# Splitting a weight tile whole instead of in two halves in a decoder step's projection queue

## The chip, the cores and the metric

The kernel runs on one core of one Trainium2 chip. The metric is device time in microseconds (us) of one execution; lower is better. Three runs of the kernel before gave a median of 2542.75 us (2541.96 to 2546.72).

## What is computed

One inference step of a two-layer decoder for 288 tokens (256 of a prompt, 32 of samples), in float32. Each layer has a token mixer and then a channel mixer. The token mixer multiplies the tokens by a wide weight matrix, runs three recurrent branches (mLSTM, GLA, SSD) on the result, projects each branch, gates and adds them, and applies an output matrix:

```python
z = jnp.matmul(x, w_in).astype(f32)
...
proj = jnp.einsum('blnc,ncd->blnd', br, w_branch.astype(f32))
gates = jax.nn.sigmoid(gate.reshape(B, L, N_BRANCH, D_MODEL))
mixed = jnp.sum(gates * proj, axis=2)
y = jnp.matmul(mixed, w_out.astype(f32))
h = _layernorm(DN_ALPHA * x.astype(f32) + y, ln1_g, ln1_b)
h = _layernorm(DN_ALPHA * h + _peer(h, p_wq, p_keys, p_u, p_v), ln2_g, ln2_b)
```

The change touches the weight matrices of the token mixer (`w_in`, `w_branch`, `w_out`). The channel mixer (`_peer`) is left as it is.

## The kernel before

A float32 product is made of three products of a shorter format. Every operand x is split into a high part (x copied into the short format, on ScalarE, L209) and a low part (x minus the high part, on VectorE, L210). TensorE adds up high times high, high times low and low times high.

The token mixers of both layers get their weights through one queue, `self.jobs`. A weight tile has 8 blocks of 128 x 128. It is loaded as a whole into a ring of `NRAW` = 3 buffers `raw` (L215, on the queue of SyncE) and used as two jobs of 4 blocks each. A layer has 83 such tiles, so 166 jobs. A job is 12 matmuls: for each block one with the high part of the weights and the high part of the tokens (L324), one with the high part of the weights and the low part of the tokens (L326), one with the low part of the weights (L328). Two jobs add up one output tile `pz` in PSUM; behind its last matmul stands `done(ps)`, which takes the output away (convolution, gate, mix and so on).

`feed()` is a generator that issues one matmul per step. The branches (`ssd`, `mlstm`, `gla`) issue their own work and call `pump(n)` in between, which takes n steps of the generator. In the mixers the engines' order is the order of issue (`tc.manual_schedule()`), so each engine works through its instructions just as this interleaving writes them; the stage after it is ordered by the planner.

At the start of job k the generator sees to it that jobs k to k + `NHI` - 1 (`NHI` = 4) are split. `hilo` splits half a tile: one buffer `hl` of the ring of four holds the high part of the half in its first 4 blocks and the low part in the last 4. `whole` splits a whole tile at once and takes two buffers of the same ring, one for the high parts of all 8 blocks and one for the low parts. The channel mixer uses `whole` (the products of `proj`, the tiles of `in_v`); the first weight tile of each layer's mixer is split as two halves by `prefetch` and `presplit`. A buffer of the ring is free again when the last matmul that reads it is done. At the end of the mixer `leave` hands the tiles that are loaded and not yet used to the channel mixer.

Names that the text uses: `convolve` (L539 to L555: two copies and one scaled copy on ScalarE, three multiply-adds on VectorE L545, and for the tile before a sigmoid L551 on ScalarE and two products L553, L555 on VectorE), `sigmoids` (L488), `gate_r` (L481), `mix` (L511, L512), `merge` (L1250, L1252, L1255).

Of the kernel before, what the change touches and what calls it, by code (L numbers as in the profile page):

```python
# [69 lines left out]
class Kernel:  # L70
# [225 lines left out]
    def add_z(self, j, done):  # L296
        self.add_x(self.I["win"][self.L, j], self.xh, self.xl, done)

    def feed(self):
        k = 0  # L300
        raws, parts = self.raws, self.parts = {}, {}
        for i, (r, p) in enumerate(self.ahead):
            raws[i] = r
            parts.update({2 * i + h: x for h, x in enumerate(p) if x})
        self.ahead = []
        ps = None
        while True:
            while k >= len(self.jobs):
                yield 0

            self.loaded = min((k + NHI) // 2 + NRAW, len(self.jobs) // 2) * 2
            for i in range(k, self.loaded):
                if i // 2 not in raws:
                    raws[i // 2] = self.load(self.jobs[i][0])
                if i < k + NHI and i not in parts:
                    parts[i] = self.hilo(raws[i // 2], i % 2)
            hi, lo = parts.pop(k)
            _, operands, done = self.jobs[k]
            first = ps is None
            if first:  # L320
                ps = self.ps_pj("pz")[:, :T]
            for m, (xh, xl) in enumerate(operands):
                last = m == 3 and done is not None
                self.pe.matmul(ps, hi[:, m], xh, start=(first and m == 0), stop=False)  # L324
                yield 1
                self.pe.matmul(ps, hi[:, m], xl, start=False, stop=False)  # L326
                yield 1
                self.pe.matmul(ps, lo[:, m], xh, start=False, stop=last)  # L328
                if last:
                    done(ps)  # L330
                    ps = None
                yield 1
            self.jobs[k] = None
            k += 1
            self.fed = k // 2
# [1507 lines left out]
```

## Time and profile before

| | |
|---|---|
| median of 3 runs | 2542.75 us (2541.96 to 2546.72) |
| the profiled execution, device time | 2553.09 us |
| its span from first to last instruction | 2551.3 us |
| TensorE (PE) busy | 2457.7 us, 96% |
| VectorE (DVE) busy | 1935.7 us, 76% |
| ScalarE (ACT) busy | 1328.5 us, 52% |
| mean granted TensorE clock | 0.979 |

The span has four stages: the mixer of layer 1 (0 to 428 us), its channel mixer (to 1264), the mixer of layer 2 (to 1696), its channel mixer (to 2551). In the timeline a row tells start, duration, engine, line, operation, what is written and read, the shape, and in brackets how long the engine sat idle before it and who released it. A row that ends in "x2" or "x4" is that many instructions behind one another, with their duration in all. Ends of matmuls are modelled.

### The profile page before, as it was taken

The numbers are of one execution on the slowest core, as the hardware profiler recorded it, in microseconds if no ns is written. First come the engines' busy times: TensorE is split into PE (matmuls) and PEld (weight loads), VectorE is DVE, ScalarE is ACT, GpSimd is POOL, SyncE is SP. The second block draws the span as 40 slices with busy tenths as digits, with TensorE's granted clock in tenths as the row PEclk, the third lists the DMA queues.
The fourth block names the chain that finished last, engine by engine and source line by source line (L and its number), as shares of the span: only waits on it lengthen the run. The fifth ranks groups of instructions, "written<-read, shape, count | busy, mean of one in ns | idle before, by whom it ended". The sixth has DMA issues, their size and how long they took to land. (4 is left out here: it accounts for less than half of the span.)

```text
span 2551.3 us, 45304 instructions
## 1 busy us (share of the span) xinstructions
PE 2457.7 (96%) x17014; PEld 2235.0 (88%) x17014; DVE 1935.7 (76%) x4156; ACT 1328.5 (52%) x2675; POOL 269.9 (11%) x270
## 2 busy tenths in 40 slices
PE   8998998989999999999999999989899999999998
PEld 8987897989999988777789888889899999878886
DVE  7667666699778868888676776767997787688885
ACT  6444765445554444444564457653455544444544
POOL 0000100240000012222000001003300000122210
PEclk9999999999999999999999989999999999999999
DMA  4422543546545568888544225434455455688883
GB/s 163 136 92 82 183 143 111 166 143 190 167 163 166 162 216 304 313 305 300 167 134 137 83 88 188 146 111 163 157 183 166 161 164 165 234 308 311 311 281 132
DMA packets 132028, 465.10 MB, mean 182 GB/s; under 512 B 15360, under 2 KB 17536, under 8 KB 131808
## 3 DMA queue, kind: packets, MB, share of 16 engines
q1 hardware_dynamic: 109728, 385.14, 45.4%
q0 software_dynamic: 22080, 77.06, 9.0%
q8 instruction: 134, 2.20, 0.3%
q14 instruction: 86, 0.70, 0.1%
HBM read 451.32 MB, written 10.82 MB: 181 GB/s over the span
## 5 line engine op out<-in xcount | busy, mean ns | idle before, releaser
L210 DVE TENSOR_TENSOR hl<-raw,hl 128x1024 fp32r<-128x1024 f32 (+1 forms) x842 | 844.8, 1008 | 393.3 <-ACT hl L209 382.5
L209 ACT ACTIVATE hl<-raw 128x1024 fp32r<-128x1024 f32 (+1 forms) x880 | 778.2, 888 | 461.4 <-PE pu L254 144.6
L1555 PE MATMUL acc<-hl,wh 128*128 128x512 f32 x2048 | 648.3, 396 | 2.6 <-ACT hl L209 1.4
L253 PE MATMUL pu<-hh,hl 128*128 128x256 f32 x2048 | 504.5, 287 | 12.4 <-ACT WA L1472 12.2
L254 PE MATMUL pu<-hl 128*128 128x256 f32 x2048 | 494.9, 280 | 0.0
L1555 PEld LDWEIGHTS acc<-hl,wh 128*128 128x128 f32 x2048 | 384.7, 188 | 100.5 <-ACT hl L209 4.9
L1555 PE MATMUL acc<-hl,wl 128*128 128x512 f32 x1024 | 404.9, 395 | 0.0
L253 PEld LDWEIGHTS pu<-hh,hl 128*128 128x128 f32 x2048 | 388.2, 190 | 14.1 <-ACT WA L1472 13.3
L254 PEld LDWEIGHTS pu<-hl 128*128 128x128 f32 x2048 | 387.8, 189 | 0.0
L326 PE MATMUL pz<-xl,hl 128*128 128x288 f32 x1008 | 325.0, 322 | 0.6 <-DVE xl L1663 0.3
L324 PE MATMUL pz<-xh,hl 128*128 128x288 f32 x1008 | 308.5, 306 | 11.8 <-ACT xh L209 6.8
L328 PE MATMUL pz<-xh,hl 128*128 128x288 f32 x1008 | 306.7, 304 | 0.0
L256 PE MATMUL pu<-hh,hl 128*128 128x256 f32 x2048 | 284.8, 282 | 2.3 <-DVE hl L210 2.3
L256 PEld LDWEIGHTS pu<-hh,hl 128*128 128x128 f32 x2048 | 260.0, 189 | 3.1 <-DVE hl L210 3.0
L1555 PEld LDWEIGHTS acc<-hl,wl 128*128 128x128 f32 x1024 | 192.5, 188 | 45.7
L209 ACT ACTIVATE wh<-WA 128x256 fp32r<-128x256 f32 x200 | 83.6, 418 | 269.1 <-PE acc L1555 266.7
L326 PEld LDWEIGHTS pz<-xl,hl 128*128 128x128 f32 x1008 | 197.4, 196 | 16.7 <-issue 11.5
L324 PEld LDWEIGHTS pz<-xh,hl 128*128 128x128 f32 x1008 | 197.6, 196 | 14.5 <-ACT xh L209 7.4
L328 PEld LDWEIGHTS pz<-xh,hl 128*128 128x128 f32 x1008 | 198.4, 197 | 3.7 <-issue 2.7
L1676 POOL DMA_INDIRECT gbuf<-in_u,se x64 | 61.7, 964 | 963.3 <-PE pu L256 701.0
L210 DVE TENSOR_TENSOR wl<-WA,wh 128x256 fp32r<-128x256 f32 x200 | 84.3, 422 | 48.4 <-ACT wh L209 48.2
L210 POOL TENSOR_TENSOR hl<-raw,hl 128x1024 fp32r<-128x1024 f32 (+1 forms) x38 | 89.6, 2357 | 188.2 <-ACT hl L209 165.6
(584 smaller groups left out, 3366.0 us busy)
## 6 DMA issues: line engine op xcount, KB each, us to landing
raw<-in_ut SPq DMA_DIRECT2D x256, 512.0 KB, 3.5
raw<-in_v SPq DMA_DIRECT2D x256, 512.0 KB, 4.7
raw<-in_win SPq DMA_DIRECT2D x126, 512.0 KB, 3.6
raw<-in_wq SPq DMA_DIRECT2D x32, 512.0 KB, 3.5
raw<-in_wbr SPq DMA_DIRECT2D x24, 512.0 KB, 3.5
raw<-in_wout SPq DMA_DIRECT2D x16, 512.0 KB, 3.6
CS<-in_C SPq DMA_DIRECT2D x16, 256.0 KB, 3.9
out_sC<-CS POOLq DMA_DIRECT2D x16, 256.0 KB, 2.8
```

The costliest lines, as they stand in the source:

```text
L209: self.ac.activation(hi, r, AF.Copy)
L210: (eng or self.ve).tensor_tensor(lo, r, hi.bitcast(F32), op=OP.subtract)
L253: self.pe.matmul(ps, wh[k], self.xh[:, k, :n], start=(k == 0), stop=False)
L254: self.pe.matmul(ps, wh[k], self.xl[:, k, :n], start=False, stop=False)
L256: self.pe.matmul(ps, wl[k], self.xh[:, k, :n], start=False, stop=(k == 7))
L324: self.pe.matmul(ps, hi[:, m], xh, start=(first and m == 0), stop=False)
L326: self.pe.matmul(ps, hi[:, m], xl, start=False, stop=False)
L328: self.pe.matmul(ps, lo[:, m], xh, start=False, stop=last)
L1555: pe.matmul(acc[t][d], lhs[:, 128 * t:128 * t + 128], rhs, start=False, stop=last and n == 2, skip_group_check=True)
L1676: self.gp.indirect_dma_start(out=g, out_offset=None, in_=src, in_offset=bass.IndirectOffsetOnAxis(ap=ix[:, r:r + 1], axis=0))
```

## The change

In `feed`, only at an even k and only for an even i, the tile of jobs i and i + 1 is split by one call of `whole` instead of two calls of `hilo` in two steps. The two jobs then get views of the two buffers: blocks 0 to 3 for job i, 4 to 7 for job i + 1. Number and order of the matmuls, of the loads and of the buffers stay.

```diff
@@ -313,7 +314,10 @@
                 if i // 2 not in raws:
                     raws[i // 2] = self.load(self.jobs[i][0])
                 if i < k + NHI and i not in parts:
-                    parts[i] = self.hilo(raws[i // 2], i % 2)
+                    if i % 2 or k % 2:
+                        continue
+                    w = self.whole(raws[i // 2])
+                    parts.update({i + h: [x[:, 4 * h:4 * h + 4] for x in w] for h in range(2)})
             hi, lo = parts.pop(k)
             _, operands, done = self.jobs[k]
             first = ps is None
```

## Rows read from the trace of the kernel before

**Rows 1.** The page: busy time of each engine; issues of weight loads.
```profile
PE 2457.7 (96%) x17014; PEld 2235.0 (88%) x17014; DVE 1935.7 (76%) x4156; ACT 1328.5 (52%) x2675; POOL 269.9 (11%) x270
...
raw<-in_win SPq DMA_DIRECT2D x126, 512.0 KB, 3.6
```
**Rows 2.** Busy time by stretch (length; PE, PEld, DVE, ACT, POOL; clock): both mixers.
```profile
0.00:428.00 428.00, 392.41 (x2811) 361.47 (x2811) 301.51 (x672) 239.97 (x548) 24.77 (x54) 0.97 0.41 133
...
1264.00:1696.00 432.00, 403.64 (x2862) 370.29 (x2860) 301.94 (x635) 248.16 (x570) 28.33 (x49) 0.95 0.40 129
```
**Rows 3.** Groups by line and shape: halves in 0:428, whole tiles in 450:1250.
```profile
L209 ACT ACTIVATE hl<-raw 128x512 fp32r<-128x512 f32 x170 | 104.4, 624 | 56.5 <-PE pz L328 48.5 <-DMA raw<-in_win 5.3 <-ACT hl L209 1.5
...
L210 DVE TENSOR_TENSOR hl<-raw,hl 128x512 fp32r<-128x512 f32 x170 | 114.5, 687 | 71.5 <-ACT hl L209 70.7
...
L209 ACT ACTIVATE hl<-raw 128x1024 fp32r<-128x1024 f32 x259 | 273.0, 1054 | 175.5 <-PE pu L254 74.4 <-issue 43.9 <-DMA raw<-in_wq 15.3
...
L210 DVE TENSOR_TENSOR hl<-raw,hl 128x1024 fp32r<-128x1024 f32 x241 | 294.8, 1224 | 114.2 <-ACT hl L209 109.3 <-ACT WA L1472 0.7 <-PE pu L256 0.5
```
**Rows 4.** Timeline of PE in the convolution stretch, layer 1.
```profile
30.96 0.29 PE L328 MATMUL pz<-xh,hl 128*128 128x288 f32 x1
...
31.36 0.29 PE L328 MATMUL pz<-xh,hl 128*128 128x288 f32 x1
...
34.54 0.30 PE L328 MATMUL pz<-xh,hl 128*128 128x288 f32 x1
```
**Rows 5.** Busy time by stretch: the convolution stretch, layer 1.
```profile
22.00:38.00 16.00, 16.00 (x121) 15.92 (x120) 15.45 (x35) 12.60 (x30) 0.00 (x0) 1.00 0.42 148
```
**Rows 6.** Timeline of ACT, then of DVE, in the same stretch.
```profile
31.29 0.39 ACT L539 ACTIVATE xp<-pz 128x256 f32<-128x256 f32 x1 [0.64 <-PE pz L328]
...
31.80 0.65 ACT L543 ACTIVATE cv<-xp,par 128x312 f32<-128x312 f32 x1
...
32.71 1.14 ACT L209 ACTIVATE hl<-raw 128x512 fp32r<-128x512 f32 x2
...
31.67 0.42 DVE L553 TENSOR_TENSOR xs<-cv,cvx 128x256 f32<-128x256 f32 x1
...
32.11 1.28 DVE L210 TENSOR_TENSOR hl<-raw,hl 128x512 fp32r<-128x512 f32 x2
33.31 1.70 DVE L545 SCALAR_TENSOR_TENSOR cv<-xp,par,cv 128x312 f32<-128x312 f32 x3
34.93 0.42 DVE L553 TENSOR_TENSOR bcs<-cv,cvx 128x256 f32<-128x256 f32 x1
```
**Rows 7.** Timeline of ACT and PE: splits behind the convolution's table load.
```profile
21.33 1.14 ACT L209 ACTIVATE hl<-raw 128x512 fp32r<-128x512 f32 x2
...
21.76 0.29 PE L328 MATMUL pz<-xh,hl 128*128 128x288 f32 x1
```
**Rows 8.** Timeline of ACT and PE: splits behind the sigmoids of the gates.
```profile
265.76 0.62 ACT L209 ACTIVATE hl<-raw 128x512 fp32r<-128x512 f32 x1
...
266.73 0.30 PE L328 MATMUL pz<-xh,hl 128*128 128x288 f32 x1
...
343.74 2.17 ACT L209 ACTIVATE hl<-raw 128x512 fp32r<-128x512 f32 x4
...
344.40 0.61 PE L324 MATMUL pz<-bmh,hl 128*128 128x288 f32 x1 [3.77 <-ACT hl L209]
...
345.13 0.61 PE L328 MATMUL pz<-bmh,hl 128*128 128x288 f32 x1
```
**Rows 9.** Timeline of DVE and PE: the split behind the last mixes.
```profile
391.34 1.29 DVE L210 TENSOR_TENSOR hl<-raw,hl 128x512 fp32r<-128x512 f32 x2
...
391.96 0.30 PE L328 MATMUL pz<-mh,hl 128*128 128x288 f32 x1
```
**Rows 10.** Timeline of DVE and PE: end of the mixer (merge).
```profile
411.75 0.69 DVE L210 TENSOR_TENSOR hl<-raw,hl 128x512 fp32r<-128x512 f32 x1 [0.21 <-ACT hl L209]
412.36 1.54 DVE L1250 SCALAR_TENSOR_TENSOR xT<-pm,xT 128x288 f32<-128x288 f32 x4
...
413.53 0.75 PE L1255 MATMUL pvar<-sqn,ones 128*128 128x288 f32 x2 [0.39 <-ACT sqn L1252]
```
**Rows 11.** Timeline of PE: SSD's first product.
```profile
55.83 0.30 PE L599 MATMUL pt<-ident,rs 128*128 128x128 f32 x1 [2.71 <-ACT rs L581]
```
**Rows 12.** Busy time by stretch: GLA and mLSTM side by side, layer 1.
```profile
176.00:236.00 60.00, 51.66 (x389) 41.89 (x389) 45.76 (x101) 24.87 (x68) 3.29 (x6) 0.91 0.21 75
```

## Prediction, made before the changed kernel was run

> **What bounds the kernel now.** I began with the page. TensorE is busy 96% of the span, VectorE 76%, ScalarE 52% [rows 1], so the end is set by matmuls one behind the other, and what the change does to the other two engines counts only where TensorE waits for them. Next came the stretches: the change acts in the two mixers alone, and there TensorE is idle for 428 - 392 = 36 us in layer 1 and 28 us in layer 2 [rows 2]. These 64 us are all that a faster split could ever give back; most of them end on the branches. Then came the shapes: a half costs 0.624 us on ScalarE and 0.687 us on VectorE, a whole tile 1.054 and 1.224 us [rows 3]. Last I went through the timeline of the mixers tile by tile and asked, at each tile, when its second half was split and when TensorE wanted the tile's first low part. That comparison decides the case, because the second half's place in the program is the place of the whole split after the change.
>
> **The change part by part.** *What goes away.* For each of about 82 tiles a layer one ScalarE and one VectorE instruction disappear. Added durations say 2 x 0.624 - 1.054 = 0.19 us saved on ScalarE and 2 x 0.687 - 1.224 = 0.15 us on VectorE [rows 3]; started back to back, two halves take VectorE 33.31 - 32.11 = 1.20 us [rows 6], so the saving there may be near nothing. Per layer that is at most 16 and 12 us of engines that mostly have room. It reaches TensorE where VectorE is full, the convolution stretch (15.45 of 16 us busy [rows 5]): six tiles at 0.15 us, at most 0.9 us a layer. I take zero.
>
> *What moves.* Before, the first half of a tile was split three jobs ahead of use and the second half three jobs ahead of its own use. Now the whole tile is split two jobs ahead: the split may start when the tile before the one in work has been used up (its two buffers come free), and has one tile's time. In clean running a tile takes TensorE 34.54 - 31.36 = 3.18 us, and the first low matmul comes 31.36 - 31.25 = 0.11 us behind the end of the tile before [rows 4], so the low part is wanted 3.29 us after its buffers come free. The split takes about 0.35 us until ScalarE has taken away the output ahead of it (one such copy lasts 0.39 us [rows 6]), then 1.05 + 0.04 + 1.22 us: 2.66 us. So 0.6 us is left, where a half had 1.59 us more time and 0.96 us less work. Any other work above 0.6 us that ScalarE or VectorE has in line ahead of the split now stops TensorE. Queued behind the waiting low split on VectorE are the branches' instructions and the next `done`; the weight load of three tiles later waits on SyncE for the same buffer, but that buffer is freed only 0.5 us later, the load lands in 3.6 us [rows 1] and is wanted 9.5 us later, so it costs nothing.
>
> *Convolution stretch.* A tile ends at 31.25. ScalarE starts on it at 31.29 and has the scaled copy at 32.45, 1.2 us behind the end [rows 4, 6]. VectorE then has the three multiply-adds, 34.93 - 33.31 = 1.62 us, two products, 32.11 - 31.67 = 0.44 us [rows 6], and now the whole low part, 1.22 us [rows 3]: 4.48 us behind the end, against 3.29 us wanted. With halves it was 1.2 + 1.62 + 0.44 + 0.69 = 3.95 us against 3.29 + 1.59 = 4.88 us, and TensorE never waited, busy 16.0 of 16 us [rows 5]. The loop closes over two tiles: two tiles take at least 4.48 + 0.04 - 0.11 + 3.18 = 7.59 us where they took 6.36, so every second tile is 1.2 us late. Six tiles stand behind convolutions; the second of them has a table load ahead of its split on ScalarE: high part from 21.33, so low part at 21.33 + 1.05 + 0.04 + 1.22 = 23.64, wanted at 21.76 [rows 7], 1.9 us late; two more are late by 1.2 us. Sum 4.3 us a layer.
>
> *Splits that come late anyway.* Behind the gates' sigmoids ScalarE reaches a split at 265.76; the low part is then there at 268.07 where TensorE wanted it at 266.73 [rows 8]: 1.4 us. At 343.74 four halves are in line; the low part comes at 346.05, wanted at 345.13 [rows 8]: 0.95 us, and the same line of four comes twice in a layer, so 1.9 us. Behind the last mixes the second half's low part began at 391.34, so its high part began at 391.34 - 0.04 - 0.62 = 390.68; the whole low part is there at 392.99, wanted at 391.96 [rows 9]: 1.05 us.
>
> *Chains that a longer split delays.* In `merge` the first tile handed to the channel mixer is now split whole ahead of the centring: its low part begins 0.43 us later and takes 0.6 us longer, so L1250 begins up to 1.0 us later than 412.36, and TensorE already waits 0.39 us for what comes of it [rows 10]: between 0 and 1.0 us, I take 0.8, since that wait shows no cover. SSD's first product waits 2.71 us for a chain through VectorE and ScalarE [rows 11]; a tile's split ahead of that chain is late by over 1 us, but hidden in the wait, and the chain itself gets 0.53 us longer (1.22 - 0.69): 0.5 us. Other tiles with less than 1 us to spare: between 0 and 3 us, I take 1.0, as most of them are late by the 0.3 us that is left between 0.6 and 0.9.
>
> *Sum.* 4.3 + 1.4 + 1.9 + 1.05 + 0.8 + 0.5 + 1.0 = 11 us a layer; layer 2 runs the same program with the same order, 2862 matmuls in 432 us [rows 2], so 22 us. The profiled execution took 2553 us, which would become 2575 us; it stands 10 us above the median of the runs, 2542.75 us, so the median becomes 2565 us. If all that is not in the convolution stretch were hidden, 9 us would stay; with the upper bounds (3.0 for the small places, 1.0 for merge, and 1.2 at SSD's start if its wait covers nothing) it is 14 us a layer, 28 us.
>
> **The rivals.** *No change.* TensorE's own waits (36 and 28 us) swallow the new ones. It needs chains that do not depend on the delayed tiles. For it: the 2.71 us at SSD's start. Against it: the convolution tiles stand ahead of every branch and delay each chain along with the matmuls. It would leave 0 to 5 us, about 2545 us.
>
> *Faster.* VectorE stood idle 71.5 us in layer 1 ahead of its 170 half splits, nearly all for ScalarE's high part [rows 3]. Half of these places go. Where GLA and mLSTM run side by side, TensorE is idle 8.3 of 60 us [rows 12] and the branches' instructions stand behind those splits. That stretch is 60/428 of the mixer: 0.5 x 71.5 x 0.14 = 5 us a layer if it all reached TensorE, and no tile were late: 10 us, 2533 us. It decides from the point at which what these chains win exceeds the new waits, 11 us a layer, so it needs most of the lateness above to be wrong too. The Trainium skill's page "Perfetto Trace Analysis", section "Optimizing Scalar/DVE Operations", speaks for it: larger operations can improve throughput if the engine is saturated, by about 60 ns an instruction on VectorE and 93 ns on ScalarE. Applied to the six tiles of the full stretch, that is an estimate of 0.4 us a layer, which the rows' 0 to 0.15 us a tile bear out. The same section says that splitting instructions up can help where these engines are not saturated but cause bubbles on others; by that rule the change goes the wrong way in most of the mixer, which is what the late tiles above come to.
>
> *Slower still.* TensorE's granted clock. In the stretch where it is often idle the mean is 0.91 [rows 12], in the full one 1.00 [rows 5]; the lower of its two levels, 1.2 against 2.4 GHz, is then granted for part of the time. If the convolution stretch and the tiles around the late splits, some 100 us a layer, fell to 0.91 too, that would be another 9 us a layer: 22 + 18 = 40 us, 2583 us.
>
> **How the numbers follow.** Forecast, slower by about 22 us (9 to 28): 0.66. Slower still, by the clock: 0.15. No change: 0.11. Faster: 0.08. A measurement of this kernel can tell about 0.2%, 5 us. So slower 0.81, same 0.11, faster 0.08. The range leaves out the faster case and the top of the clock's: 2546 to 2581 us.
>
> **What would show it.** In the profile after, the group of the split is 128x1024 in the mixers too, some 164 fewer instructions on either engine. In the stretch from 20 to 45 us TensorE has gaps ahead of L328 (low part, released by VectorE L210) of about 1.9, 1.2 and 1.2 us, which were not there; the groups L324 and L328 of `pz` show idle time ended by `hl`, together some 15 to 20 us. Each mixer is 9 to 14 us longer, the channel mixers unchanged. Wrong would be: no gaps at L328 in the convolution stretch (then the two-tile loop is wrong), gaps but no later end of the mixer (absorbed), or a shorter stretch at 176 to 236 us (the queue on VectorE was worth more than thought).

## The result and the profile after

The changed kernel took 2585.64 us (median; 2581.28 to 2587.13), the kernel before 2544.73 us (2541.96 to 2553.18): ratio 1.0146, 95% interval 1.0125 to 1.0168. Slower was right; 2565 us was not, and 2585.64 us lies above the range. Beside the experiments the kernel before was run many more times, with medians of 2547.5 to 2548.9 us, so the change costs 37 to 41 us.

The page of the kernel after, the lines that answer to [rows 1, 3, 4]. The lines of the feed stand four lower than before, so L332 is the matmul with the low part that was L328, and L328 the one that was L324. In a group, "|" is followed by busy time, mean ns of one, and the idle time ahead with what ended it.

```profile
PE 2464.9 (96%) x17014; PEld 2239.7 (87%) x17014; DVE 1920.8 (74%) x3988; ACT 1300.8 (50%) x2507; POOL 264.0 (10%) x270
...
L210 DVE TENSOR_TENSOR hl<-raw,hl 128x1024 fp32r<-128x1024 f32 (+1 forms) x674 | 823.6, 1223 | 394.1 <-ACT hl L209 376.7
...
L332 PE MATMUL pz<-xh,hl 128*128 128x288 f32 x1008 | 308.0, 306 | 13.1 <-DVE hl L210 13.1
L328 PE MATMUL pz<-xh,hl 128*128 128x288 f32 x1008 | 306.8, 304 | 9.7 <-ACT xh L209 5.9
```

VectorE and ScalarE issue 168 instructions fewer each and are busy 15 and 28 us less, yet the time rose. In the group L332 TensorE now waits 13.1 us for low parts. The same group on the page of the kernel before had no wait:

```profile
L328 PE MATMUL pz<-xh,hl 128*128 128x288 f32 x1008 | 306.7, 304 | 0.0
```

In the convolution stretch, where it never stopped [rows 5], the timeline of PE of the kernel after has these waits in layer 1 (the first three of four; in brackets the idle time and who ended it):

```profile
16.62 0.40 PE L332 MATMUL pz<-xh,hl 128*128 128x288 f32 x1 [0.53 <-DVE hl L210]
...
21.06 0.40 PE L332 MATMUL pz<-xh,hl 128*128 128x288 f32 x1 [0.73 <-DVE hl L210]
...
28.81 0.40 PE L332 MATMUL pz<-xh,hl 128*128 128x288 f32 x1 [0.98 <-DVE hl L210]
```

To see where the rest went I cut each mixer at the ends of tiles 0, 13, 53 and 82, so that each stretch holds the same matmuls in every kernel. First come the busy times by stretch of the kernel after (columns as in [rows 2]; three stretches of layer 1, then three of layer 2), then those of the kernel before with two buffer counts lowered, which is the control of the experiments and took the same time as the kernel before.

```profile
12.45:65.29 52.84, 45.99 (x319) 43.59 (x318) 40.26 (x94) 28.92 (x52) 0.00 (x0) 0.97 0.42 130
65.29:313.80 248.51, 232.49 (x1695) 206.33 (x1695) 161.40 (x327) 122.64 (x270) 13.82 (x25) 0.95 0.38 115
313.80:432.44 118.64, 109.32 (x765) 106.12 (x765) 78.41 (x135) 65.08 (x123) 3.77 (x7) 0.96 0.46 148
1299.46:1349.65 50.19, 44.76 (x319) 42.39 (x318) 35.06 (x61) 29.00 (x52) 0.00 (x0) 1.00 0.45 137
1349.65:1597.50 247.85, 231.95 (x1695) 206.33 (x1695) 156.14 (x296) 122.58 (x270) 13.83 (x25) 0.95 0.38 115
1597.50:1716.00 118.50, 109.19 (x765) 105.98 (x765) 78.40 (x135) 65.11 (x123) 3.78 (x7) 0.96 0.47 148
```

```profile
14.28:61.08 46.80, 44.06 (x319) 43.66 (x318) 40.57 (x107) 30.52 (x65) 0.00 (x0) 0.96 0.46 147
61.08:298.83 237.75, 224.35 (x1695) 200.56 (x1695) 165.92 (x368) 127.64 (x309) 13.85 (x25) 0.99 0.39 120
298.83:412.32 113.49, 108.10 (x765) 104.92 (x765) 81.09 (x164) 70.05 (x151) 3.78 (x7) 0.97 0.47 155
1280.71:1324.70 43.99, 42.57 (x319) 42.16 (x318) 35.10 (x76) 30.48 (x65) 0.00 (x0) 1.00 0.48 154
1324.70:1568.70 244.00, 230.57 (x1695) 205.74 (x1695) 161.21 (x338) 127.99 (x309) 13.87 (x25) 0.96 0.37 118
1568.70:1682.14 113.44, 108.05 (x765) 104.87 (x765) 81.08 (x164) 70.04 (x151) 3.79 (x7) 0.97 0.48 155
```

The lengths add up to 836.5 us after and 799.5 us in the control: 37.1 us. The rest of the span is 6.0 us shorter in the profile after (spans 2579.4 and 2548.3 us), so it is partly chance that this agrees so well with the 37 us of the medians. Length less TensorE's busy time is its idle time: 62.8 against 41.8 us, 21.1 us more. The other 16.0 us are the same matmuls taking longer. Part of that belongs to the waits: a matmul is drawn 0.29 us long and the next begins 0.13 us behind it [rows 4], so at a wait the last one still counts as busy for 0.16 us, and the one behind it takes 0.40 us; a wait costs some 0.27 us more than its bracket says. The rest is the granted clock: in these stretches the trace has its lower level, 1.2 GHz, for 44 us in the control, 61 us in the profile of before and 72 us after. The same cut through the profile of the kernel before gives 802.4 us, 37.4 of it idle. By stretch, both layers together:

| us | tiles 1 to 13 | tiles 14 to 53 | tiles 54 to 82 | sum |
|---|---|---|---|---|
| control | 90.8 | 481.8 | 226.9 | 799.5 |
| the profiled execution of before | 91.3 | 485.4 | 225.8 | 802.4 |
| after | 103.0 | 496.4 | 237.1 | 836.5 |
| predicted to be added | 9.6 | 4.8 | 7.5 | 21.9 |
| added, against the control | 12.2 | 14.6 | 10.2 | 37.1 |
| added, against before | 11.7 | 11.0 | 11.4 | 34.1 |

The middle, where the branches run, is where the added time is furthest from the forecast. Two things are in it: longer waits for the branches' chains of instructions, and slower matmuls. One chain shows the first. These are rows of ACT, DVE and PE from the timeline of the kernel before, then of the kernel after: GLA's state update, for which TensorE waits at `pr`. The bracket of the last row tells how long TensorE was idle and for what.

```profile
282.90 0.41 ACT L474 ACTIVATE gate<-pz 128x288 f32<-128x288 f32 x1 [1.85 <-PE pz L328]
283.20 0.62 ACT L209 ACTIVATE hl<-raw 128x512 fp32r<-128x512 f32 x1
...
283.86 0.69 DVE L210 TENSOR_TENSOR hl<-raw,hl 128x512 fp32r<-128x512 f32 x1 [2.09 <-ACT hl L209]
284.47 0.68 DVE L924 TENSOR_TENSOR CS<-CS,ec 128x512 f32<-128x512 f32 x1
...
285.26 0.69 DVE L925 TENSOR_TENSOR CS<-CS,pc__3121 128x512 f32<-128x512 f32 x1
...
286.09 1.10 PE L1173 MATMUL pr<-sq,ones 128*128 128x512 f32 x2 [0.42 <-DVE CS L925]
```

```profile
290.62 0.41 ACT L478 ACTIVATE gate<-pz 128x288 f32<-128x288 f32 x1 [3.23 <-PE pz L332]
290.93 1.05 ACT L209 ACTIVATE hl<-raw 128x1024 fp32r<-128x1024 f32 x1
...
292.01 1.23 DVE L210 TENSOR_TENSOR hl<-raw,hl 128x1024 fp32r<-128x1024 f32 x1 [6.19 <-ACT hl L209]
293.15 0.69 DVE L928 TENSOR_TENSOR CS<-CS,ec 128x512 f32<-128x512 f32 x1
293.94 0.69 DVE L929 TENSOR_TENSOR CS<-CS,pc__3019 128x512 f32<-128x512 f32 x1
...
294.78 1.10 PE L1177 MATMUL pr<-sq,ones 128*128 128x512 f32 x2 [1.39 <-DVE CS L929]
```

From the gate's copy to `pr` it was 286.09 - 282.90 = 3.19 us and is 294.78 - 290.62 = 4.16 us: 0.97 us more. That is the longer split on ScalarE, 1.05 - 0.62 = 0.43 us, and on VectorE, 1.23 - 0.69 = 0.54 us. No weight was late here. The branch's own instruction stood in VectorE's line behind a split, the split behind ScalarE's, and TensorE's wait grew by the difference, 0.42 to 1.39 us. The wait for `hr` in mLSTM grew alike; before, then after, from the timelines of PE:

```profile
195.28 0.31 PE L1024 MATMUL pa<-X 64*32 64x32 f32 x6 [2.63 <-DVE hr L929]
```

```profile
200.38 0.42 PE L1028 MATMUL pa<-X 64*32 64x32 f32 x6 [3.58 <-DVE hr L933]
```

Not every wait grew. Against the control, seven waits for chains in the middle of layer 1 grew, by 5.0 us together, and five shrank, by 3.5 us; layer 2 has the same twelve, with nearly the same sums. With the waits for splits, TensorE's idle time in the middle grew by 2.6 us in layer 1 and by 2.5 us in layer 2.

The second thing is the clock. In the kernel after it fell to 1.2 GHz during this wait for `hr` and stayed there for 13.7 us in either layer; in the control it fell some 2 us behind the wait, for 3.4 us in layer 1 and 10.2 us in layer 2. The rows of layer 1 by stretch, after, then control (the clock is the number 0.50):

```profile
199.70:213.35 13.65, 12.97 (x56) 10.18 (x58) 8.35 (x19) 2.89 (x7) 1.61 (x3) 0.50 0.22 78
```

```profile
194.70:198.10 3.40, 3.40 (x16) 2.74 (x13) 2.52 (x8) 1.84 (x6) 0.00 (x0) 0.50 0.02 5
```

In the whole middle, both layers, the clock was at 1.2 GHz for 48 us after and for 27 us in the control; but for 48 us also in the profile of before, so this share moves from one execution to the next.

### The profile page after: what moved, and what is told of

The parts are those of the page before. It is cut to its first block, busy times and chain, and to the rows that moved or that the text cites. A ratio compares the mean times of both kernels' runs of the same rounds, so it can differ in the third digit from the quotient of the medians.

```text
span 2579.4 us, 44779 instructions
## 1 busy us (share of the span) xinstructions
PE 2464.9 (96%) x17014; PEld 2239.7 (87%) x17014; DVE 1920.8 (74%) x3988; ACT 1300.8 (50%) x2507; POOL 264.0 (10%) x270
## 5 line engine op out<-in xcount | busy, mean ns | idle before, releaser
L210 DVE TENSOR_TENSOR hl<-raw,hl 128x1024 fp32r<-128x1024 f32 (+1 forms) x674 | 823.6, 1223 | 394.1 <-ACT hl L209 376.7
L209 ACT ACTIVATE hl<-raw 128x1024 fp32r<-128x1024 f32 (+1 forms) x712 | 747.2, 1050 | 405.5 <-PE pu L254 145.7
L253 PE MATMUL pu<-hh,hl 128*128 128x256 f32 x2048 | 504.7, 287 | 10.2 <-ACT WA L1476 10.0
L332 PE MATMUL pz<-xh,hl 128*128 128x288 f32 x1008 | 308.0, 306 | 13.1 <-DVE hl L210 13.1
L328 PE MATMUL pz<-xh,hl 128*128 128x288 f32 x1008 | 306.8, 304 | 9.7 <-ACT xh L209 5.9
L332 PEld LDWEIGHTS pz<-xh,hl 128*128 128x128 f32 x1008 | 196.7, 195 | 22.4 <-DVE hl L210 18.2
L328 PEld LDWEIGHTS pz<-xh,hl 128*128 128x128 f32 x1008 | 196.3, 195 | 11.9 <-ACT xh L209 5.9
```

What stands on the lines that cost most here:

```text
L209: self.ac.activation(hi, r, AF.Copy)
L210: (eng or self.ve).tensor_tensor(lo, r, hi.bitcast(F32), op=OP.subtract)
L253: self.pe.matmul(ps, wh[k], self.xh[:, k, :n], start=(k == 0), stop=False)
```

## Experiments

Two theories stood against each other. **LATE**: the low part of a whole split is there after TensorE wants it. **LINE**: the longer split stands in the lines of ScalarE and VectorE ahead of branch instructions that TensorE waits for, whether or not a weight is late. Each kernel's time is a median beside the kernel before on the same chip; "first", "middle" and "last" are tiles 1 to 13, 14 to 53 and 54 to 82 of both layers, against the control, from one profile each. That such a figure moves by some us from one execution to the next is seen in the row of before in the table (3.6 us in the middle).

**Where does it cost?** e1, e2 and e3 split whole in one range of tiles only: 1 to 13, 14 to 53 (the diff), and from 54 on.

```diff
-                    parts[i] = self.hilo(raws[i // 2], i % 2)
+                    if 14 <= i // 2 < 54:
+                        if i % 2 or k % 2:
+                            continue
+                        w = self.whole(raws[i // 2])
+                        parts.update({i + h: [x[:, 4 * h:4 * h + 4] for x in w] for h in range(2)})
+                    else:
+                        parts[i] = self.hilo(raws[i // 2], i % 2)
```

> Only tiles 1 to 13 of each layer (convolution, SSD's start) are split whole, the rest in halves. Two theories. LATE: a whole split has one tile's time and more work, so the low part comes after TensorE wants it; by the terms of the prediction tiles 1 to 13 cost 4.3 + 0.9 = 5 us a layer, 10 us in all: 2555 us. LINE: beside that, the longer split stands in ScalarE's and VectorE's line ahead of instructions of the branches that TensorE waits for; there are few of these so early, so also 10 to 12 us. If the convolution loop is not the cause, no change: 2545 us.

> Only tiles 14 to 53 of each layer (the three branches side by side) are split whole. LATE: by the prediction 1.4 us behind the sigmoids and 1 us of small places, 2.4 us a layer: 2550 us. LINE: each wait of TensorE for a branch that has a whole split ahead of it on VectorE grows by 0.43 + 0.53 = 0.96 us, some five or six of these a layer, so 6 us a layer and more: 2557 us or more.

> Only tiles 54 to 82 of each layer and what is handed to the channel mixer are split whole. LATE: 1.9 us behind the two lines of four splits, 1.05 us behind the last mixes, 0.8 us in merge, 3.75 us a layer: 2552 us. LINE adds nothing here, since the branches are over. If parts add up, the three times of e1 to e3 above the kernel before make up the 37 to 41 us that the whole change costs.

Measured: e1 2559.76, e2 2569.2, e3 2559.84 us, beside 2548.59: ratios 1.0048 (1.003 to 1.0066), 1.0085 (1.0057 to 1.0114), 1.0039 (1.0023 to 1.0055). That is 11, 21 and 11 us; 43 together, against 37 for all at once, which the intervals (4 to 7 us either way for each part) do not tell apart. Each adds its time in its own stretch: e1 12.3 in the first, e2 17.4 in the middle, e3 10.0 in the last. In e1's profile the middle is 6.2 us shorter, all of it in layer 2 (237.8 us for the control's 244.0; in layer 1 237.8 for 237.7), where the control had the clock at 1.2 GHz for 20 us and e1 for 14 us. So this does not show that the branches' waits swallow the convolution's delay: 12.3 us were added there in the profile, and the medians differ by 11 us. The middle, with the smallest share in the prediction, has the largest.

**Halves at the whole split's place (e4).** Both halves of a tile are split at the even job, two jobs ahead, as two instructions on each engine.

```diff
                 if i < k + NHI and i not in parts:
+                    if k % 2:
+                        continue
                     parts[i] = self.hilo(raws[i // 2], i % 2)
```

> All tiles in halves, but both halves are split in the step where the change splits the whole tile (even jobs only): the lead of the change without the long instructions. LATE: the first half's low part is ready 0.96 us sooner than a whole one, so the convolution loop is late by 0.25 us a tile instead of 1.2 us in two tiles, the other late places cost nothing or little: 3 us a layer, 2551 us. LINE: two halves behind one another hold VectorE (1.20 us against 1.14) and ScalarE as long as a whole one, so the branches' waits grow all the same by about 6 us a layer: 2560 us or more.

Measured: 2570.97 us, ratio 1.0086 (1.0064 to 1.0108). First 6.5, middle 12.6, last 2.7 us. The first low part is ready one half sooner, which gives back half of the convolution's loss and most of the last stretch's; the middle stays, since the lines are as long as with the whole split. For LINE there, for LATE at both ends.

**More lead.** The control e5 has fewer buffers elsewhere, to make room; e6 and e7 have two more split buffers on top and split one tile earlier, e6 whole, e7 in halves. The first cut is from e5, the second from e6, both against the kernel before.

```diff
 NGATE = 12
-NW2 = 12
-NROW = 8
+NW2 = 10
+NROW = 5
```

```diff
+    def ring(self, t):
+        pool, tag, n = (self.mx, "hm", 2) if t % 3 == 1 and t < 83 else (self.stream, "hl", NHI)
+        return pool.tile([128, 8, 128], F32R, tag=tag, name="hl", bufs=n)
...
-                if i < k + NHI and i not in parts:
-                    parts[i] = self.hilo(raws[i // 2], i % 2)
+                if i < k + (6 if i < 166 else 4) and i not in parts:
+                    if i % 2 or k % 2:
+                        continue
+                    w = [self.ring(i // 2) for _ in range(2)]
+                    self.split(raws[i // 2], *w)
...
```

> The kernel before with 10 buffers w2 instead of 12 and 5 row buffers instead of 8, which makes room for the next two. Control: 2545 us, or up to 10 us more where a branch waits for a buffer.

> The control with two more split buffers, and every tile split whole one tile earlier (four jobs ahead of use instead of two). LATE: the low part is there in time everywhere, TensorE's gaps for it go, and the time is that of the control within 5 us. LINE: the long instructions stand in the same engines' lines as before, so the branches' longer waits stay, some 6 us a layer: 12 us above the control.

> The control with two more split buffers, tiles in halves, each half split five jobs ahead instead of three. LATE: where halves are late in the kernel before (behind the sigmoids, two lines of four), up to 3 us a layer come back: 0 to 6 us below the control. LINE: the same as the control.

Measured: control 2548.62 us, ratio 1.0000 (0.9987 to 1.0014); e6 2571.57 us, 1.0104 (1.0084 to 1.0124); e7 2556.91 us, 1.0042 (1.0023 to 1.006). With a tile more of lead, e6 has no wait in the convolution stretch, and of the change's 37 us 14 come back; 23 stay, 3.9 in the first stretch, 11.6 in the middle, 7.4 in the last. The chains wait as long as in the kernel after; rows of PE from e6's timeline:

```profile
197.18 0.42 PE L1032 MATMUL pa<-X 64*32 64x32 f32 x6 [3.60 <-DVE hr L937]
...
290.07 1.10 PE L1181 MATMUL pr<-sq,ones 128*128 128x512 f32 x2 [1.38 <-DVE CS L933]
```

So 14 us come back with the lead, or up to 22 if the 8 us that e7 loses by its lead are in e6 too. That is not all of LATE: in e6's last stretch TensorE still waits longer for splits than in the control, by 0.43 and 0.41 us at `bmh` and by 0.43 and 0.54 us at `bgh` in each layer. Lead with halves won nothing, against what was expected of e7; 5.0 of its 8 us lie in the last stretch, and why is open.

**Only the low part in pieces.** In e8 the changed kernel's low part is two instructions in the same step; in e9 the second of them is issued a job later. e9 also issues each load a job later (a line not shown here); its trace has no split on ScalarE that waited for a load.

```diff
-                    w = self.whole(raws[i // 2])
+                    w = [self.stream.tile([128, 8, 128], F32R, tag="hl", name="hl", bufs=NHI) for _ in range(2)]
+                    self.ac.activation(w[0], raws[i // 2], AF.Copy)
+                    for h in range(2):
+                        s = slice(4 * h, 4 * h + 4)
+                        self.ve.tensor_tensor(w[1][:, s], raws[i // 2][:, s], w[0][:, s].bitcast(F32), op=OP.subtract)
```

```diff
...
+            if k % 2 and rest:
+                self.low(*rest)
...
+                    self.low(r, w, 0)
+                    if i == k:
+                        self.low(r, w, 1)
+                    else:
+                        rest = r, w, 1
```

> The changed kernel, but VectorE makes the low part of a tile in two instructions of half a tile each, behind one whole high part. LATE: the low part that TensorE wants first is there 0.53 us sooner, so a third to a half of the cost goes: 2570 us. LINE: VectorE and ScalarE are held as long as before (1.20 against 1.14 us), the branches' waits stay; if these are the larger part, 2580 us or more.

> The changed kernel, but VectorE makes the low part in two halves, the second one a job later (in the odd step), so that 0.6 us instead of 1.14 us stand in VectorE's line at one place; the high part stays whole. LINE, now the larger part of the cost: each branch wait that grew by 0.43 (high part) + 0.53 (low part) grows by 0.43 alone, and the convolution loop is late by 0.6 instead of 1.2 us: 2565 to 2570 us against 2585. If VectorE's line is not the cause (ScalarE's whole high part, or the lead alone), it stays at 2580 us or more.

Measured: e8 2582.07 us, ratio 1.0147 (1.0125 to 1.0168); e9 2572.1 us, 1.0091 (1.0062 to 1.012). By stretch e8 has first 9.4, middle 21.8, last 4.4 us, e9 8.4, 16.2 and 3.5 us. Two pieces in one place win nothing that can be measured: TensorE gets its first low part sooner (first stretch 9.4 instead of 12.2), but the line is as long as before. With the second piece a job later about 13 us come back against the change, and 10 us against e8. TensorE's idle time that ended on anything but a split is 36.4 us in tiles 1 to 82 of e8 and 21.7 us in e9, so the other waits did fall, as LINE has it. These two runs speak for the length of what stands in one place, not the number of instructions. But in e9's profile the middle is no shorter than the change's (16.2 against 14.6 us): the same matmuls took longer there, with the clock at 1.2 GHz for 68 us where the change has 48.

**Shorter pieces than halves (e10).** The kernel before with each half split as two quarters, the second in the middle of the job.

```diff
...
+                    self.quarter(raws[i // 2], parts[i], i % 2, 0)
+                    if i < k + NHI - 1:
+                        self.quarter(raws[i // 2], parts[i], i % 2, 1)
+                    else:
+                        rest = raws[i // 2], parts[i], i % 2, 1
...
+                if m == 2 and rest:
+                    self.quarter(*rest)
+                    rest = None
```

> The other way round: the kernel before with every half split in two quarters, the second one issued in the middle of the job. LINE: each branch wait with a split ahead of it in line falls by up to 0.4 us, 3 us a layer, 2543 us; but 0.15 us more VectorE time a half, which in the convolution stretch (VectorE full) costs 2 us a layer: 2543 to 2550 us. LATE: more work in the same lead, nothing to win: 2549 to 2556 us.

Measured: 2575.75 us, ratio 1.0111 (1.0082 to 1.0141): slower by 28 us. Of 23.0 us added by its profile the middle has 18.7. The sum of TensorE's idle time in the six stretches went up by 4.6 us only (822.5 - 776.1 = 46.4 us against 41.8), its busy time by 18.4 us at the same matmuls. In the row of its stretch from tile 13 to 53 in layer 1 the clock is 0.94 where the control has 0.99; the first row is one of the times at half speed in it, around the wait for `hr`:

```profile
188.10:201.76 13.66, 12.78 (x54) 9.98 (x56) 8.45 (x23) 2.86 (x9) 1.62 (x3) 0.50 0.11 44
58.09:308.54 250.45, 235.08 (x1694) 210.15 (x1694) 173.94 (x452) 135.80 (x389) 13.82 (x25) 0.94 0.37 116
```

Neither theory had this loss. Some waits for chains did fall as LINE expected (`pr` from 0.41 us to 0, `ident,mk` from 1.11 to 0.83 us in layer 1). But in the middle of either layer TensorE waited 2.47 and 3.09 us for a load of state, which it did in no other kernel; the row of PE for layer 1:

```profile
303.71 0.50 PE L1159 MATMUL pos<-QS,SS 128*128 128x8 f32 x3 [2.47 <-DMA SS<-in_S]
```

So e10 also moved a load, and is no clean test of shorter pieces.

The Trainium skill, page "Perfetto Trace Analysis", section "Optimizing Scalar/DVE Operations", says that breaking up instructions may let work be completed sooner where VectorE and ScalarE are not saturated but cause bubbles. The runs bear it out between whole tiles and halves; between halves and quarters they do not, with the late load of e10 in it.

**The line by itself (e11).** The kernel before, with one idle VectorE instruction of a half's size behind the second half's split of tiles 14 to 82. Nothing reads its output; the result and the place of all splits stay.

```diff
                     parts[i] = self.hilo(raws[i // 2], i % 2)
+                    if i % 2 and 14 <= i // 2 < 83:
+                        st = self.mx.tile([128, 6], F32, tag="idle", name="idle", bufs=1)
+                        self.ve.bn_stats(st, raws[i // 2][:, 4:].rearrange("p k c -> p (k c)"))
```

> The kernel before, in halves, but behind the second half's split of tiles 14 to 82 VectorE has one more instruction of 128x512 (0.7 us) whose result nobody reads: VectorE's line is as long at that place as with a whole split, while no part of a tile comes later. LINE: the branches' waits grow by 0.6 us each, about 4 us a layer: 2556 us or more. LATE: nothing waits for it, 2549 us.

Measured: 2580.91 us, ratio 1.0131 (1.0102 to 1.0161), 33 us, nearly the loss of the change, though every weight is split where it was before: first 0.1, middle 23.5, last 6.2 us. The rows of DVE from its timeline are the chain shown above, with the idle instruction in it, then PE's:

```profile
288.08 0.69 DVE L210 TENSOR_TENSOR hl<-raw,hl 128x512 fp32r<-128x512 f32 x1 [2.10 <-ACT hl L209]
288.69 0.69 DVE L319 BATCH_NORM_STATS2 idle<-raw 128x6 f32<-128x512 f32 x1
289.29 0.67 DVE L927 TENSOR_TENSOR CS<-CS,ec 128x512 f32<-128x512 f32 x1
290.07 0.69 DVE L928 TENSOR_TENSOR CS<-CS,pc__3197 128x512 f32<-128x512 f32 x1
...
290.90 1.10 PE L1176 MATMUL pr<-sq,ones 128*128 128x512 f32 x2 [1.01 <-DVE CS L928]
```

The wait is 1.01 us where it was 0.42: the 0.60 us by which L927 stands behind the idle instruction's start. TensorE's idle time that ended on a split is 10.0 us in tiles 1 to 82, as in the control, so no part came later; all the added idle time ended on something else. In the last stretch that is `mix` (L514), 0.26 to 0.92 us at six places a layer, where the expectation of e3 had LINE add nothing. VectorE is 78% busy in this kernel; room on the whole did not help the chains. So LINE alone can cost about as much as the whole change. But of the 23.5 us in the middle only 6.1 are idle time; 17.4 are the same matmuls taking longer, with the clock at 1.2 GHz for 65 us where the control had 27.

**The line made shorter (e12).** The kernel before, with the low part of the first halves of tiles 14 to 53 made by GpSimd (POOL).

```diff
-                    parts[i] = self.hilo(raws[i // 2], i % 2)
+                    parts[i] = self.hilo(raws[i // 2], i % 2, self.gp if 14 <= i // 2 < 54 and i % 2 == 0 else None)
```

> The kernel before (halves), with one thing moved: the low part of the first half of tiles 14 to 53 is made by GpSimd (POOL) instead of VectorE, 40 instructions a layer. GpSimd is nearly idle in the mixers (24.8 of 428 us) and has a first half's low part three jobs ahead of its use. LINE (what stands in VectorE's line ahead of the branches' instructions counts): VectorE's line gets shorter by 40 x 0.69 = 27 us a layer just where a longer line cost 6 us a layer, so the time falls by 3 to 8 us: 2540 to 2546 us beside 2548. LATE (only a part that comes after TensorE wants it counts): no part was late in the kernel before, so nothing is won, 2548 us; and if GpSimd takes over 4.9 us for a half, or stands with it behind other work, the first halves come late and it is slower by 5 us or more, with gaps ahead of L328 that end on POOL.

Measured: 2556.31 us, ratio 1.0029 (1.0013 to 1.0045), 8 us slower where LINE had expected 3 to 8 us faster. 80 instructions of 0.687 us were taken from VectorE, 55 us, but its busy time fell by 17 us only, from 1935.7 to 1918.8. The rows of DVE and POOL from its timeline, then the same DVE line in the kernel before:

```profile
181.97 2.26 DVE L883 TENSOR_TENSOR qn<-qe,nP 128x512 f32<-128x512 f32 x1
...
182.38 1.29 POOL L210 TENSOR_TENSOR hl<-raw,hl 128x512 fp32r<-128x512 f32 x1
```

```profile
183.63 0.69 DVE L883 TENSOR_TENSOR qn<-qe,nP 128x512 f32<-128x512 f32 x1
```

An instruction of VectorE beside a split of GpSimd takes 2.26 us where it took 0.69: the line got longer at just these places. The Trainium skill, page "SBUF — State Buffer", section "SBUF: two separate sides", says that VectorE instructions with two inputs in SBUF and GpSimd's lock each other out of one shared pair of ports for the whole instruction; these rows agree in the sum, 0.69 + 1.29 = 1.98 us of the 2.26. By the rows VectorE's instruction began 0.41 us ahead of GpSimd's and was yet the one that took longer, which that sentence does not tell. VectorE's own half splits beside one of GpSimd, 16 of them, took 1.19 us on average for 0.69 us. So e12 did not make the line shorter, and decides nothing between the theories. None of the kernels beat the kernel before.

**What TensorE's time went to.** The traces tell what ended each idle time of TensorE and which clock was granted. Tiles 1 to 82 of both layers, one execution of each kernel:

| us | control | before | after | e6 | e10 | e11 |
|---|---|---|---|---|---|---|
| idle, ended by a split (`hl`) | 10.0 | 10.0 | 30.2 | 13.6 | 13.3 | 10.0 |
| idle, ended by anything else | 31.8 | 27.4 | 32.6 | 37.2 | 33.1 | 44.3 |
| clock at 1.2 GHz | 44 | 61 | 72 | 82 | 82 | 75 |

In the change itself 20.2 of the 21.1 us of added idle time ended on a split; the chains' longer and shorter waits cancel to 0.8 us. Where lateness is mostly gone (e6) or absent (e11), the other waits are 5.4 and 12.5 us longer. So LATE and LINE need not be two shares that add up to the 37 us: in the change waits for splits took the place of waits for chains. How the 37 us divide between them stays open.

The clock's part can be estimated from all executions on record. Its mean is 0.9815 in 52 executions of the kernel before and 0.977 in the four of the kernel after. At two levels, 0.5 and 1, a mean 0.0045 lower is 2 x 0.0045 x 2580 = 23 us more at 1.2 GHz, and if the matmuls do half their work in that time, it costs at most 12 us. Among the 52 executions, the seven at 0.979 or below (0.978 on average) took 2551.9 us and the five at 0.984 took 2544.2 us: 8 us for 0.006, so 6 us for 0.0045. By this estimate 6 to 12 of the 37 us are the clock's; for e11 (0.9745) 9 to 18 of 33 us, for e10 (0.972) 13 to 24 of 28 us. No run set the clock by itself, so what made it fall is not shown.

## Why the prediction was right and wrong

**Right: what bounds it, and the late splits.** The two-tile loop of the convolution stretch holds. By the ends of tiles 1 to 11 it costs 4.2 us in layer 1 and 4.6 us in layer 2 against the profile of before, for 4.3 us predicted; but as four stalls of about 1.1 us, not one of 1.9 and two of 1.2. The one behind the table load is no longer than the others, so there the sum came out by two errors. Behind the sigmoids 1.4 us was predicted and 1.4 us measured at tile 46, of which tile 47 gave back 0.5; 0.95 us for the first line of four and 0.7 us measured at tile 63 in layer 1; 1.05 us behind the last mixes and 0.9 us at tile 76; 0.8 us for `merge` and 0.56 us at tile 82. With a tile more of lead (e6) the convolution's waits are gone, so the mechanism is shown, not only the sum. Idle time ended by `hl` at the matmuls of `pz` was to be 15 to 20 us: those with the low part have 16.6 us (0.4 before) and the first ones with the high part 13.6 us (9.6 before), 20.2 us more. The channel mixers are 1.5 and 2.3 us shorter than in the profile of before. Even the sum of the waits comes near against the control: 21.1 us of idle time were added, by stretch 8.1, 5.1 and 7.8 us, where 9.6, 4.8 and 7.5 us, 21.9 in all, were forecast; the 0.27 us at each new wait come on top. In the middle that is luck, as the next but one paragraph shows.

**Wrong: the pace of the matmuls, held fixed.** This is the step that failed. The sum adds up waits and leaves the matmuls at their pace; the clock stood beside it as a case of 0.15 with 18 us more, 2583 us in all, close to what came. Measured, 16.0 of the 37.1 us are the same matmuls taking longer (against the profile of before 8.7 of 34.1 us): the 0.27 us at each new wait, and the clock, 6 to 12 us by the estimate above. The change cost 15 us more than the 22 us forecast; that is 6 to 12 of them, and the rest lies with the term of the next paragraph. The clock was no separate case but a further term, and not where that case had it: the convolution stretch runs on at full clock, 1.00 in layer 2. One place is plain. At `bgh` the waits grew from 1.02 and 0.20 to 1.44 and 0.73 us, 0.95 us as predicted for the second line of four, and behind them the clock went to 1.2 GHz, which it did not in the kernel before; two rows of PE and the stretch behind them in the kernel after:

```profile
385.34 0.40 PE L328 MATMUL pz<-bgh,hl 128*128 128x288 f32 x1 [1.44 <-ACT hl L209]
...
386.60 0.40 PE L332 MATMUL pz<-bgh,hl 128*128 128x288 f32 x1 [0.73 <-DVE hl L210]
```

```profile
387.44:390.86 3.42, 3.42 (x16) 3.42 (x15) 1.16 (x3) 0.44 (x1) 0.00 (x0) 0.50 0.84 284
```

TensorE is busy all of the 3.42 us, at half speed; the tile's end is 2.5 us later in either layer, 1.5 us beyond the waits. How much the clock took in the middle depends on what one compares with: against the control TensorE's busy time there is 9.5 us longer and its idle time 5.1 us, against the profile of before, which had been at 1.2 GHz as long as the kernel after, 1.6 and 9.4 us. Before and control do the same work in the same median time, and differ there by 8 us of busy time in the one execution of each that was profiled. By either, the middle's 4.8 us were 6 to 10 us too few.

**Wrong, and half hidden: the term for the small places, under "Chains that a longer split delays".** It asked which other tiles come late by the lack of lead and took 1.0 us a layer, between 0 and 3. The split's greater length ahead of a chain was counted at two places only, SSD's start and `merge`. It holds at more places where TensorE waits for a chain with a split in its line. Control against after, layer 1: `hr` 2.63 to 3.58 us, `ident,mk` 1.11 to 1.63, `pr` 0.80 to 1.11 and 0.41 to 1.39, `bsh` 1.28 to 1.94, `ident,mv` 0.03 to 0.56, `St` 0.33 to 1.42: the 5.0 us named above, beyond the upper bound, and none of these waits is for a weight. The term did not have the 3.5 us of waits that shrank either, so that against the control the middle's idle time came out at 2.6 us a layer where 1.4 + 1.0 us stood; against the profile of before it is 4.7 us a layer. SSD's start and the two tiles around it, 0.5 us in the sum, cost 1.3 and 1.6 us. That the lines do this without any late weight is shown by e11, and that the longer waits stay when most of the lateness is taken away by e6.

**Wrong: the base.** Of the 21 us between 2565 and 2585.64 us, 6 are the base: three runs gave 2542.75 us, 52 executions 2548.6 us. The sum itself was made on one execution of 2553 us, which had spent 3.6 us more in the middle than the control; against it the change adds 34.1 us, against the control 37.1 us.

**The rivals.** No change is refuted as a whole, but its mechanism is there in small: the wait at SSD's start fell from 2.71 to 1.91 us behind a new wait of 1.42 us for a split, and five waits a layer shrank in the middle. Faster is refuted: a whole low part holds VectorE's line for 293.15 - 292.01 = 1.14 us, two halves for 1.20 us [rows 6], so 0.06 us a tile is all that a full line could win, and the 15 us saved on VectorE and the places that went from its line bought nothing, because what is left at each place is longer. In the middle VectorE's busy time fell from the control's 327 us to 318 and the stretch got 14.6 us longer.

## What to carry to other kernels

Before two instructions are merged, list not only who waits for their result but whose instructions stand behind them on the same engine: every chain that the bounding engine waits for can grow by the added length, on each engine it passes, here by up to 0.43 + 0.54 us a place. Waits do not simply add up: here those that grew in the middle by 5.0 us a layer stood beside others that shrank by 3.5 us. An engine at 76% can be the one whose order decides, and saving it time does not shorten a line whose pieces get longer. Where a sum of waits is made for an engine with a varying clock, the clock belongs in the sum as a term with a range, not beside it as an unlikely case.

## What the hardware showed that was not expected

A VectorE instruction of 128x512 with both inputs in SBUF took 2.26 us instead of 0.69 us beside a GpSimd instruction of 1.29 us (e12), so work moved to the idle GpSimd came back on VectorE: 38 of the 55 us moved away. The same half took GpSimd 1.29 us and VectorE 0.69 us. And a kernel can lose 28 us with hardly more waiting (e10): 18.4 of the 23 us that its profiled execution added in the mixers were longer busy time of the same matmuls, with a granted clock of 0.94 for 0.99 in the row shown and a mean of 0.972 for 0.9815 over the executions; which difference in the waits, the late load among them, brought that about was not tried.
